# Keys and values of the first sequence finished at the attention's entry, a pool laid out first, and fewer column products ahead of and within the S5 tables

## The chip, the cores and the metric

The kernel runs on one NeuronCore of a Trainium2 chip. The metric is the device time of one execution in microseconds (us). The engines are named as in the profile: PE is TensorE (matmuls and transposes; PEld is its weight load), DVE is VectorE, ACT is ScalarE, POOL is GpSimd, and SP is SyncE, which here only issues transfers. Each engine works through its own queue in order. A transfer is issued by SP, ACT or POOL and runs on the core's 16 DMA engines.

## The reference

One encoder layer over two sequences of 512 tokens, width 1024, in float32. Each branch reads a normalized input; the two are gated and merged, and a squared-ReLU MLP follows.

```python
h = rms_norm(x, ln1)
q, k, v, u, g_att, g_ssm = jnp.split(h @ w_in, IN_SPLITS, axis=-1)   # 1024, 256, 256, 1024, 1024, 1024 columns
q = rms_norm(q.reshape(bsz, seq_len, 16, 64), q_gain)
k = rms_norm(k.reshape(bsz, seq_len, 4, 64), k_gain)
v = v.reshape(bsz, seq_len, 4, 64)
y_att = windowed_attention(q, k, v, sink, bias, mask)   # blocks of 128 queries, 3 blocks of keys, 16 heads on 4 key heads
y_ssm = s5_branch(u, ...)    # 64 groups of 16 channels, 64 complex states, forward and backward scan, then GELU and a gate
mixed = sigmoid(g_att) * y_att + sigmoid(g_ssm) * y_ssm
x = x + mixed @ w_out
return x + square(relu(rms_norm(x, ln2) @ w_up)) @ w_down
```

## The kernel before, in words

Every large product is made of three passes over operands that are split into a high part (a cast) and a low part (the difference): high by high, high by low, low by high. ScalarE makes the high part and VectorE the low one.

The part around the change has these stages, in order of time.

1. *Start (0 to about 60 us).* Keys and values of the first sequence are projected with the very first weights (strip_products) and stored, raw apart from the row's norm, in kv_scr (scaled_heads). The tokens are turned into hT. VectorE works out the powers pr and pi of the state matrix, which lie in the pool ssmc; the input rows, strips and bias line lie in the pool xin. From the powers, ScalarE and VectorE copy the arranged tables br_p, bi_p, er, ei (L518 to L526), and VectorE adds bs_p and es.
2. *Tables (to about 215 us).* tables(c) handles eight groups, in two steps of four. A step computes bpre (VectorE), turns it on TensorE (L608) into bm, computes ctab, and multiplies bm with the inputs u (L637), which fills the state array h. all_lags makes the Toeplitz lags.
3. *Recurrence (to about 358 us).* 62 steps of four VectorE operations (L737 to L740).
4. *Outputs (to about 430 us).* 32 quarter steps of small products (L771, L774) and a GELU.
5. *Attention's entry (about 441 to 470 us).* Four query tiles of the first head group are projected, and the values of the second sequence; the keys are turned. Then come the attention units.

Between these, TensorE is fed with the columns of the big projection (u and the two gates: 24 columns of 48 products of 128x512) and the second sequence's keys (96 products of 128x256). They stand in one generator; pull(n) issues the next n units of it at that place of TensorE's queue. A column product counts 2 units, a key product 1. Where the reserve "phase["units"] - 84" stands, so many units are left for after the last output. Each column's weights are cast (L182, c_hi) and subtracted (L183, c_lo) during the column before; the load of the next pair of raw halves (L172, c_raw) goes out once both are done. A gate column that ends in or before the recurrence gets its sigmoid with its evacuation; a later one gets a copy, and its sigmoid in a later stage.

During the recurrence the kernel also finishes the first sequence's keys and values, one block of 128 tokens after the other, in head_piece: from step 24 on, every second step, three pieces a block. Piece 0 loads the block from kv_scr (SP). Piece 1 squares the keys and casts the values (ScalarE), subtracts (POOL) and stores the values to v_scr (POOL's queue). Piece 2 reduces the squares (VectorE), adds the epsilon, takes the power -0.5 and scales the keys (POOL) and stores them to k_scr. Its three tiles per block (kv, kv_sq, va_t) share one ring of three slots:

```python
kv, sq = [sp.tile([P, 2, N_KV, HD], F32, tag="ys", name=n, bufs=3) for n in ("kv", "kv_sq")]
va_t = sp.tile([P, N_KV, P], F32R, tag="ys", name="va_t", bufs=3)
```

At the attention's entry, SP loads the finished keys (kn) and values (va), POOL copies the first head's keys twice side by side (kd, key_copies), and key_turn turns them after the first query tile. A query tile is projected, squared (ScalarE), reduced (VectorE), raised to -0.5 (POOL, power), scaled (VectorE, norm) and turned by TensorE one tile later; rows_block projects values between. Three PSUM banks ("acc") go round among projection, value rows and turned tile.

The order of work: in the start, all five engines follow the written order (manual_schedule). In the tables only TensorE and POOL do, VectorE, ScalarE and SP are ordered by a planner. In recurrence and outputs TensorE, ScalarE and VectorE follow the written order, POOL and SP the planner's. At the attention's entry only VectorE does. Pools lie on a stack: what is opened after a pool is closed takes its place in memory, and waits for it, tile by tile if the closed pool says reuse_waits="tile" (xin does, ssmc does not). The pools hst (the state array h) and ssmt (the tables' tiles, among them bcx, the coefficients that SP loads for each tables(c)) take the place of xin and ssmc. The line "line_scr" (L707) spreads the 16 bias lines over 128 partitions in DRAM; POOL issues it, after the loads of the first Toeplitz and output tables.

Of the kernel before, what the change touches and what calls it, by code (L numbers as in the profile page):

```python
# [19 lines left out]
P = 128  # L20
# [6 lines left out]
HALF = 512  # L27
# [36 lines left out]
def hybrid_layer(ctx, tc, x, x_t, w_kv, rel, onehot, w_qkv, w_ug, vectors, lam, coefs, w_glu, w_out, ln2,  # L64
# [39 lines left out]
    k_scr = dram.tile([P, NB, N_KV, HD], F32, name="k_scr")  # L104
    v_scr = dram.tile([P, NB, N_KV, P], F32, name="v_scr")
# [179 lines left out]
    with tc.tile_pool(name="xin", bufs=1, reuse_waits="tile") as xin, tc.tile_pool(name="ssmc", bufs=1) as sc:  # L285
# [232 lines left out]
        for src, e_t, b_t, eng in ((pr, er, br_p, S.copy), (pi, ei, bi_p, V.tensor_copy)):  # L518
            bt = b_t.rearrange("p g t -> p t g")
            eng(bt[0:64], src[0:64, 7::-1, :])  # L520
            eng(bt[64:128], src[64:128, 0:8, :])
# [7 lines left out]
        V.tensor_add(es, er, ei)  # L529
# [3 lines left out]
    with tc.tile_pool(name="hst", bufs=1) as hp:  # L533
# [11 lines left out]
        with tc.tile_pool(name="ssmt", bufs=2) as sp:  # L545
# [9 lines left out]
            def tables(c):  # L555
# [18 lines left out]
                for q in range(SB // SG):  # L574
# [40 lines left out]

                    tb = sp.tile([P, SG, 9, CH], F32, tag="tb", name="tb", bufs=1)
# [29 lines left out]
                    pull(48 if g0 + SG < GROUPS else 36)  # L646
# [21 lines left out]
            pull(96)  # L668
# [12 lines left out]
        with tc.tile_pool(name="ssmo", bufs=2) as sp:  # L681
# [28 lines left out]
            pieces = {}  # L710

            def head_piece(t, i):
                if i == 0:
                    kv, sq = [sp.tile([P, 2, N_KV, HD], F32, tag="ys", name=n, bufs=3) for n in ("kv", "kv_sq")]
                    va_t = sp.tile([P, N_KV, P], F32R, tag="ys", name="va_t", bufs=3)
                    pieces[t] = kv, sq[:, 0], va_t
                    SP.dma_start(kv, kv_scr[:, t])
                    return
                kv, sq, va_t = pieces[t]
                if i == 1:  # L720
                    S.activation(sq, kv[:, 0], AF.Square, scale=HD ** -0.5)
                    S.copy(va_t[:, :, 0:HD], kv[:, 1])
                    GP.tensor_tensor(va_t[:, :, HD:P], kv[:, 1], va_t[:, :, 0:HD].bitcast(F32), op=ALU.subtract)
                    GP.dma_start(v_scr[:, t], va_t.bitcast(F32))
                    return
                ms, rk = [small.tile([P, N_KV], F32, tag=tag, name=tag) for tag in ("ms", "rq")]
                V.reduce_sum(ms, sq, axis=AX.X)
                GP.tensor_scalar_add(ms, ms, EPS)
                GP.tensor_tensor(rk, ms, neg_half[:, 0:N_KV], op=ALU.pow)
                GP.tensor_tensor(kv[:, 0], kv[:, 0], rk[:, :, None].to_broadcast([P, N_KV, HD]), op=ALU.mult)  # L730
                GP.dma_start(k_scr[:, t], kv[:, 0])

            for i in range(1, NCHUNK - 1):
                if i >= 24 and i % 2 == 0 and (i - 24) % 8 < 6 and (i - 24) // 8 < NB:
                    head_piece((i - 24) // 8, (i - 24) % 8 // 2)
                t1, t2 = terms if i == 1 else [step_tile(n) for n in ("t1", "t2")]
                V.tensor_mul(t1, h[:, i], a8r)  # L737
                V.tensor_mul(t2, h[:, i, ::-1], a8i)
                V.tensor_add(t1, t1, h[:, i + 1])
                V.tensor_add(h[:, i + 1], t1, t2)  # L740
                pull(15)
# [19 lines left out]
            for q in range(GROUPS // SH):  # L761
# [23 lines left out]
                pull(-(-(phase["units"] - 84) // (GROUPS // SH - q)))  # L785
# [74 lines left out]
    with tc.tile_pool(name="att", bufs=2, reuse_waits="tile") as ap, tc.tile_pool(name="attc", bufs=1, reuse_waits="tile") as ac:  # L860
# [51 lines left out]

        def key_turn(j, sq, kd):
            kh = ap.tile([P, HALF], F32R, tag="kh", name="kh")
            kl = ap.tile([P, HALF], F32R, tag="kl", name="kl")
            keys[j, sq] = (kh, kl)
            ps = tps()
            for t in range(4):
                PE.transpose(ps[:, t * P:(t + 1) * P], kd[:, t].rearrange("p a d -> p (a d)"), ident)
            S.activation(kh, ps, AF.Copy, scale=gain_k)  # L920
            V.scalar_tensor_tensor(kl, ps, gain_k, kh.bitcast(F32), op0=ALU.mult, op1=ALU.subtract)
            queries[j, sq] = ap.tile([P, G, HALF], F32R, tag="qa", name="qa")
# [191 lines left out]
        with tc.manual_schedule(engines={ET.DVE}):  # L1114
            SP.dma_start(kn[:, 0:4], k_scr)
            kd = key_copies(0, 0)
            w_q = whole_block(w_qkv[Q_BLK], wq, "ya", 2)
            weights[0] = w_q
            w_v = whole_block(w_qkv[V_BLK], cpool, "p", 3)
            last_keys.pop()()  # L1120
            SP.dma_start(kn[:, 4:8], key_tiles[0])
            load_biases(0)
            SP.dma_start(va[:, 0:4].bitcast(F32), v_scr)
            rows = None
            for t in range(4):
                new = Tile(0, 0, t)
                new.project(3 * KT)
                new.square()
                new.power()
                new.norm()  # L1130
                if rows:
                    rows.turn()
                    rows.high()
                    rows.low()
                rows = new
                rows_block(w_v, NB + t, v_evac)
                if t == 0:
                    key_turn(0, 0, kd)
# [661 lines left out]
```

## Time and profile before

| what | value |
| --- | --- |
| median of 3 runs | 1485.83 us (1483.88 to 1486.2) |
| the profiled execution, whole | 1483.64 us |
| its span, first to last instruction | 1481.9 us |
| TensorE busy | 1441.8 us, 97% |
| VectorE busy | 1100.2 us, 74% |
| ScalarE busy | 765.2 us, 52% |
| GpSimd busy | 247.8 us, 17% |
| mean granted TensorE clock | 0.990 |

A group's row reads: line, engine, operation, output and inputs, shapes, count, then busy time and mean duration of one in ns, then idle time of the engine ahead of it and what ended it. A row of the timeline reads: start, duration, engine, line, operation, with idle time and releaser in brackets. A row of the waits reads: who, for whom, total us, times, longest. A row of a stretch reads: from and to, length, then busy time and instructions of each engine, then the granted clock of TensorE as a share of full speed, the DMA engines' busy share and GB/s. Matmul durations overlap in the rows, since they are pipelined; the spacing of their starts is their cost.

### The profile page before, as it was taken

To read this page: it belongs to the slowest core of one execution; us is meant where nothing else is said; L and a number is where in the kernel's file an instruction comes from. 1 tells how busy PE (TensorE), PEld (TensorE's weight loads), DVE (VectorE), ACT (ScalarE), POOL (GpSimd) and SP (SyncE) were. 2 spreads that over 40 slices of the span, in tenths; PEclk is the share of its full clock that TensorE was granted. 3 is DMA by queue.
4 is the path that set the end of the run, shared out by engine and by line. 5 is a ranking of instruction groups with operands and counts; after the bars stand their busy time and mean duration, and the time that the engine had idled before them with its cause. 6 is when DMAs were issued, how large, how long until landed. Compare 5 with 4: busy or idle time off the path is not lost.

```text
span 1481.9 us, 22085 instructions
## 1 busy us (share of the span) xinstructions
PE 1441.8 (97%) x7981; PEld 1227.5 (83%) x7981; DVE 1100.2 (74%) x1985; ACT 765.2 (52%) x1367; POOL 247.8 (17%) x408
## 2 busy tenths in 40 slices
PE   8899999779999999999999999999999999999998
PEld 7688888568999999987888878888888888888887
DVE  7889949678545899998995479777776588575653
ACT  7578872123435888787353255544444443433332
POOL 3034441322423433243100000000000000000000
PEclk9999999989999999999999999999999999999999
DMA  7255546653981342255554234444443794454441
GB/s 289 94 162 165 164 143 227 222 181 123 320 288 67 124 148 87 70 163 177 184 171 155 87 129 170 157 156 150 156 156 114 289 342 140 148 182 157 128 127 58
DMA packets 102524, 243.38 MB, mean 164 GB/s; under 512 B 12522, under 2 KB 24298, under 8 KB 102288
## 3 DMA queue, kind: packets, MB, share of 16 engines
q1 hardware_dynamic: 61968, 141.25, 29.4%
q0 software_dynamic: 16832, 49.86, 10.2%
q10 hardware_dynamic: 23616, 50.87, 9.3%
q8 instruction: 63, 1.03, 0.3%
q14 instruction: 45, 0.37, 0.1%
HBM read 170.60 MB, written 83.39 MB: 171 GB/s over the span
## 4 chain that ended last, share of the span: by engine, by line
PE 65%; DVE 8%; ACT 3%; DMA 2%; issue 2%; POOL 1%; SPq 0%; DVEq 0%; ACTq 0%; POOLq 0%
PE bank L123 13%; PE bank L124 13%; PE bank L125 13%; PE acc L937 5%; PE acc L125 2%; PE acc L123 2%; PE acc L124 2%; PE acc L130 2%; PE sps L774 2%; PE po L1020 2%; PE acc L192 2%; PE sps L988 2%; PE tps L1004 2%; DMA k_scr<-kv 1%; PE sps L771 1%
## 5 line engine op out<-in xcount | busy, mean ns | idle before, releaser
L192 PE MATMUL acc<-act,c_hi 128*128 128x512 f32 x768 | 245.6, 400 | 19.5 <-ACT c_hi L182 19.5
L192 PEld LDWEIGHTS acc<-act,c_hi 128*128 128x128 f32 x768 | 142.7, 191 | 48.0 <-ACT c_hi L182 20.3
L124 PE MATMUL bank<-b_lo,a_hi 128*128 128x512 f32 (+1 forms) x449 | 174.4, 389 | 0.0
L125 PE MATMUL bank<-b_hi,a_lo 128*128 128x512 f32 (+1 forms) x449 | 174.4, 389 | 0.0
L123 PE MATMUL bank<-b_hi,a_hi 128*128 128x512 f32 (+1 forms) x449 | 174.4, 389 | 0.0
L192 PE MATMUL acc<-act,c_lo 128*128 128x512 f32 x384 | 151.7, 395 | 0.2 <-DVE c_lo L183 0.2
L1656 ACT CAST a_hi<-d_a 128x1024 fp32r<-128x1024 f32 x56 | 59.0, 1054 | 177.3 <-PE bank L124 174.1
L123 PE MATMUL bank<-act,act 128*128 128x512 f32 x368 | 143.2, 389 | 0.3 <-DVE tx L1444 0.3
L124 PE MATMUL bank<-act,act 128*128 128x512 f32 x368 | 143.2, 389 | 0.0
L125 PE MATMUL bank<-act,act 128*128 128x512 f32 x368 | 143.2, 389 | 0.0
L1657 DVE TENSOR_TENSOR a_lo<-d_a,a_hi 128x1024 fp32r<-128x1024 f32 x56 | 68.5, 1223 | 95.9 <-ACT a_hi L1656 95.9
L937 PE MATMUL acc<-w_hi,act 128*128 128x256 f32 x512 | 114.2, 291 | 0.7 <-ACT w_hi L1108 0.7
L125 PEld LDWEIGHTS bank<-b_hi,a_lo 128*128 128x128 f32 x449 | 84.3, 188 | 17.5
L123 PEld LDWEIGHTS bank<-b_hi,a_hi 128*128 128x128 f32 x449 | 84.3, 188 | 17.4
L124 PEld LDWEIGHTS bank<-b_lo,a_hi 128*128 128x128 f32 x449 | 84.3, 188 | 17.3
L937 PEld LDWEIGHTS acc<-w_hi,act 128*128 128x128 f32 x512 | 87.0, 189 | 4.6 <-ACT w_hi L1108 0.9
L192 PEld LDWEIGHTS acc<-act,c_lo 128*128 128x128 f32 x384 | 73.0, 190 | 16.0 <-DVE c_lo L183 1.0
L998 ACT ACTIVATE p<-p,nmx 128x257 f32<-128x257 f32 (+1 forms) x128 | 72.1, 564 | 19.7 <-DVE nmx L992 17.4
L123 PEld LDWEIGHTS bank<-act,act 128*128 128x128 f32 x368 | 69.1, 188 | 15.0 <-issue 0.6
L130 PE MATMUL acc<-act,gc_hi 128*128 128x512 f32 x256 | 81.0, 394 | 0.0
L124 PEld LDWEIGHTS bank<-act,act 128*128 128x128 f32 x368 | 69.1, 188 | 14.4
L125 PEld LDWEIGHTS bank<-act,act 128*128 128x128 f32 x368 | 69.1, 188 | 14.2
(358 smaller groups left out, 3434.6 us busy)
## 6 DMA issues: line engine op xcount, KB each, us to landing
d_a<-a_scr SPq DMA_DIRECT2D x56, 512.0 KB, 3.6
raws<-in_w_up_dram SPq DMA_DIRECT2D x32, 512.0 KB, 4.0
a_scr<-t ACTq DMA_DIRECT2D x64, 256.0 KB, 2.8
k<-in_w_down_dram SPq DMA_DIRECT2D x32, 512.0 KB, 6.4
c_raw<-in_w_ug_dram SPq DMA_DIRECT2D x48, 256.0 KB, 3.7
ct_scr<-ctab POOLq DMA_DIRECT2D x16, 512.0 KB, 4.4
ctab_in<-ct_scr POOLq DMA_DIRECT2D x16, 512.0 KB, 7.1
a_scr<-a ACTq DMA_DIRECT2D x32, 256.0 KB, 2.0
```

Of the source, the lines that this page charges most:

```text
L123: PE.matmul(ps, a[0], b[0], start=first, stop=False)
L124: PE.matmul(ps, a[0], b[1], start=False, stop=False)
L125: PE.matmul(ps, a[1], b[0], start=False, stop=last)
L130: PE.matmul(ps, w[wi][:, k, :], rows[yi], start=k + p == 0, stop=k == KT - 1 and p == 2)
L192: PE.matmul(ps, w[wi][:, k, :], hT[s][hi][:, k, :], start=n == 0, stop=n == 3 * KT - 1)
L774: PE.matmul(o, ctab[:, g0 % SI + g, ri, 0:T * CH], st[:, ri, g].rearrange("p s k -> p (s k)"), start=False, stop=ri == 1)
L937: PE.matmul(self.ps, hT[sq][act][:, k, col:col + P], w[:, k % 4, :], start=i == 0, stop=i == 3 * KT - 1)
L988: PE.matmul(ps[:, 0:self.nk], qs, kk[:, self.k0 * P:self.k1 * P], start=i == 0, stop=i == 1)
L998: S.activation(p, p, AF.Exp, bias=self.nmx[:, h:h + 1], scale=-1.0, accum_out=self.sums[:, h, self.qb:self.qb + 1])
L1004: PE.transpose(pt[:, h * P:(h + 1) * P], self.p[:, h, 1 + i * P:1 + (i + 1) * P], ident)
L1656: S.copy(hi, src)
L1657: V.tensor_sub(lo, src, hi.bitcast(F32))
```

## The change

The pieces in the recurrence, k_scr and v_scr go. At the attention's entry the raw keys and values come straight from kv_scr: the four blocks' keys are squared, reduced, raised and scaled in one operation each, the values cast and subtracted in one each; the copy kd moves behind the first tile's value rows, and key_turn behind the third's. The pool ssmc is opened ahead of xin, so that it lies below it. The arranging copies are dealt anew (ScalarE gives one half of br_p to VectorE), and es is added in the first step of the tables. The pulls become 72 for 96 ahead of the tables and 44 for 48 in fifteen of their sixteen steps; the reserve behind the outputs becomes 100 for 84.

```diff
-    k_scr = dram.tile([P, NB, N_KV, HD], F32, name="k_scr")
-    v_scr = dram.tile([P, NB, N_KV, P], F32, name="v_scr")
...
-    with tc.tile_pool(name="xin", bufs=1, reuse_waits="tile") as xin, tc.tile_pool(name="ssmc", bufs=1) as sc:
+    with tc.tile_pool(name="ssmc", bufs=1) as sc, tc.tile_pool(name="xin", bufs=1, reuse_waits="tile") as xin:
...
-        for src, e_t, b_t, eng in ((pr, er, br_p, S.copy), (pi, ei, bi_p, V.tensor_copy)):
+        for src, b_t, engs in ((pr, br_p, (S.copy, V.tensor_copy)), (pi, bi_p, (V.tensor_copy,) * 2)):
             bt = b_t.rearrange("p g t -> p t g")
-            eng(bt[0:64], src[0:64, 7::-1, :])
-            eng(bt[64:128], src[64:128, 0:8, :])
+            engs[0](bt[0:64], src[0:64, 7::-1, :])
+            engs[1](bt[64:128], src[64:128, 0:8, :])
...
-        V.tensor_add(es, er, ei)
...
+                    if g0 == 0:
+                        V.tensor_add(es, er, ei)
                     tb = sp.tile([P, SG, 9, CH], F32, tag="tb", name="tb", bufs=1)
...
-                    pull(48 if g0 + SG < GROUPS else 36)
+                    pull(44 if g0 + SG < GROUPS else 36)
...
-            pull(96)
+            pull(72)
...
-            def head_piece(t, i):
...
             for i in range(1, NCHUNK - 1):
-                if i >= 24 and i % 2 == 0 and (i - 24) % 8 < 6 and (i - 24) // 8 < NB:
-                    head_piece((i - 24) // 8, (i - 24) % 8 // 2)
...
-                pull(-(-(phase["units"] - 84) // (GROUPS // SH - q)))
+                pull(-(-(phase["units"] - 100) // (GROUPS // SH - q)))
...
+        def query_tile(j, sq):
+            if (j, sq) not in queries:
+                queries[j, sq] = ap.tile([P, G, HALF], F32R, tag="qa", name="qa")
...
-            SP.dma_start(kn[:, 0:4], k_scr)
-            kd = key_copies(0, 0)
+            SP.dma_start(kn[:, 0:4], kv_scr[:, :, 0])
...
-            SP.dma_start(va[:, 0:4].bitcast(F32), v_scr)
+            vn = ap.tile([P, NB, N_KV, HD], F32, tag="p", name="vn", bufs=3)
+            SP.dma_start(vn, kv_scr[:, :, 1])
+            k_sq = evp.tile([P, NB, N_KV, HD], F32, tag="ev", name="k_sq")
+            ms, rk = [small.tile([P, NB * N_KV], F32, tag="rsum", name=n, bufs=2) for n in ("k_ms", "k_rs")]
+            query_tile(0, 0)
             rows = None
             for t in range(4):
                 new = Tile(0, 0, t)
                 new.project(3 * KT)
+                if t == 0:
+                    S.activation(k_sq, kn[:, 0:4], AF.Square, scale=HD ** -0.5)
+                    V.reduce_sum(ms, k_sq.rearrange("p t h d -> p (t h) d"), axis=AX.X)
+                    GP.tensor_scalar_add(ms, ms, EPS)
+                    GP.tensor_tensor(rk, ms, neg_half, op=ALU.pow)
                 new.square()
                 new.power()
                 new.norm()
...
                 rows_block(w_v, NB + t, v_evac)
                 if t == 0:
+                    V.tensor_mul(kn[:, 0:4], kn[:, 0:4],
+                                 rk.rearrange("p (t h) -> p t h", t=NB)[:, :, :, None].to_broadcast([P, NB, N_KV, HD]))
+                    kd = key_copies(0, 0)
+                if t == 1:
+                    S.copy(va[:, 0:4, :, 0:HD], vn)
+                    V.tensor_sub(va[:, 0:4, :, HD:P], vn, va[:, 0:4, :, 0:HD].bitcast(F32))
+                if t == 2:
                     key_turn(0, 0, kd)
```

More of the change, by code (lines that the diff above doesn't have):

```diff
@@ L709, in hybrid_layer @@
             order.enter_context(tc.manual_schedule(engines={mybir.EngineType.PE, mybir.EngineType.Activation, mybir.EngineType.DVE}))
-            pieces = {}
-            def head_piece(t, i):
[L713 to L731, printed above, removed]
             for i in range(1, NCHUNK - 1):
-                if i >= 24 and i % 2 == 0 and (i - 24) % 8 < 6 and (i - 24) // 8 < NB:
-                    head_piece((i - 24) // 8, (i - 24) % 8 // 2)
                 t1, t2 = terms if i == 1 else [step_tile(n) for n in ("t1", "t2")]
@@ L921, in key_turn @@
             V.scalar_tensor_tensor(kl, ps, gain_k, kh.bitcast(F32), op0=ALU.mult, op1=ALU.subtract)
-            queries[j, sq] = ap.tile([P, G, HALF], F32R, tag="qa", name="qa")
+            query_tile(j, sq)
         class Tile:
```

## The prediction

> **What bounds the kernel now.** I read the page first: TensorE is nearly the whole span, so only its gaps, and the time it runs at half clock, can be won; work that merely moves along its queue wins nothing. The waits of TensorE come next (total, times, longest, in us).
>
> ```profile
> PE 1441.8 (97%) x7981; PEld 1227.5 (83%) x7981; DVE 1100.2 (74%) x1985; ACT 765.2 (52%) x1367; POOL 247.8 (17%) x408
> ...
> PE acc L192 <- ACT c_hi L182: 19.5, 2, 18.9
> PE tps L608 <- issue: 3.7, 1, 3.7
> ...
> PE sps L774 <- ACT st L750: 0.9, 1, 0.9
> ...
> PE acc L937 <- ACT w_hi L1108: 0.7, 1, 0.7
> ...
> PE acc L937 <- DVE w_lo L1109: 0.3, 1, 0.3
> ```
>
> One wait is 18.9 us. The timeline around it, one piece of the chain that ended last, and the table of transfers say what it is:
>
> ```profile
> 272.49 0.41 DVE L727 TENSOR_REDUCE ms<-kv_sq 128x4 f32<-128x256 f32 x1
> 273.00 0.32 POOL L728 TENSOR_SCALAR ms<-ms 128x4 f32<-128x4 f32 x1 [11.78 <-DVE ms L727]
> ...
> 285.83 0.39 PE L192 MATMUL acc<-act,c_lo 128*128 128x512 f32 x1
> 285.90 1.05 POOL L707 DMA_DIRECT2D line_scr<-line_one  x1 [1.39 <-DMA u_sb<-u_scr]
> ...
> 289.02 0.62 POOL L731 DMA_DIRECT2D k_scr<-kv  x1 [0.30 <-POOL kv L730]
> ...
> 304.17 0.40 ACT L722 CAST va_t<-kv 128x256 fp32r<-128x256 f32 x1 [25.86 <-DMA k_scr<-kv]
> 305.13 1.41 DVE L183 TENSOR_TENSOR c_lo<-c_raw,c_hi 128x512 fp32r<-128x512 f32 x2 [20.14 <-ACT c_hi L182]
> ...
> 289.02 15.07 DMA k_scr<-kv
> ...
> line_scr<-line_one POOLq DMA_DIRECT2D x1, 4096.0 KB, 17.9
> ```
>
> The second head piece's cast (va_t) waits for a slot of the three-deep "ys" ring, held until the first piece's keys are stored. That store left POOL at 289.02, behind the 4 MB bias-line copy of 285.90, and took 15.07 us. ScalarE runs in order, so the column weights' cast c_hi stood behind va_t; TensorE stopped for want of c_hi, and VectorE for the same reason (20.14 us). The next view gives busy time by engine, then granted clock, in four stretches.
>
> ```profile
> 289.53:305.05 15.52, 0.00 (x0) 0.00 (x0) 0.00 (x0) 0.88 (x3) 0.50 (x2) 0.50 0.86 299
> 305.05:310.01 4.96, 4.86 (x12) 3.66 (x13) 4.78 (x12) 2.17 (x5) 2.32 (x5) 0.50 0.58 199
> 65.30:68.95 3.65, 0.00 (x0) 0.03 (x1) 2.83 (x6) 3.03 (x11) 0.00 (x0) 0.82 0.56 186
> 224.25:285.00 60.75, 60.75 (x270) 50.30 (x269) 58.17 (x147) 11.77 (x21) 14.68 (x22) 1.00 0.60 197
> ```
>
> After the stop TensorE ran 4.96 us at clock 0.50. The last row gives the price of a column product: 60.75 us by 270 is 0.225 us.
>
> **The change, part by part.** All sums are against the profiled execution's own 1483.64 us (span 1481.9); the median of the runs, 1485.83, stands 2.2 above it.
>
> *Head pieces out of the recurrence.* Gone are four SP loads, eight ScalarE, four VectorE and sixteen POOL operations, and eight POOL stores. No ring slot waits for a store any more, so the 18.9 us stop goes, and with it the half clock behind it, worth half of 4.96: 2.5 us. Together 21.4. What is late next? VectorE's recurrence runs beside these products; it gains 20.14 us of idle time and the reduces:
>
> ```profile
> L727 DVE TENSOR_REDUCE ms<-kv_sq 128x4 f32<-128x256 f32 x3 | 1.2, 411 | 0.0
> ```
>
> That is 21.3, as much as TensorE gains, so the two arrive together at the outputs as before; of the 0.9 us wait on st there I take 0.5 as won (between 0 and 0.9). POOL is no longer held until VectorE's reduce of 272.49, so the table loads and the bias-line copy go out earlier, beside the column loads (a rival below).
>
> *Fewer columns ahead.* The 24 units ahead of the tables are 12 products, the 4 units in 15 steps are 30: 42 products, 9.5 us, move into the output stage, where TensorE works without gaps as well. By itself nothing (one half column's sigmoid more falls to the later stage, on a ScalarE that is busy for 52% of the span), provided that the tables still cover VectorE. Seven pairs of steps from 80.42 to 204.37 sum to:
>
> ```profile
> sum 123.95, PE 123.95 PEld 108.31 DVE 112.51 ACT 101.55 POOL 54.90; mean PE 17.71 PEld 15.47 DVE 16.07 ACT 14.51 POOL 7.84
> ...
> 88.81 1.28 DVE L598 TENSOR_TENSOR bpre<-tb,bpre 128x512 f32<-128x512 f32 x2
> ...
> 89.98 1.04 PE L608 MATMUL tps<-ident,bpre 128*128 128x128 f32 x8
> ```
>
> A pair takes TensorE 17.71 us; four products fewer make it 16.81, still over VectorE's 16.07. Only the third step has no slack (VectorE ends at 90.09, the transposes start at 89.98); it may lose up to 1.8 (two steps' 0.9, doubled for a late one). I take 0, since VectorE also starts earlier, by the next part.
>
> *Powers' pool first, copies dealt anew, es later.*
>
> ```profile
> 55.04 1.16 ACT L521 COPY br_p<-pr 64x512 f32<-64x512 f32 x1
> ...
> 56.78 0.66 DVE L520 COPY bi_p<-pi 64x512 f32<-64x512 f32 x1
> ...
> 58.23 0.69 DVE L522 TENSOR_TENSOR bs_p<-br_p,bi_p 128x512 f32<-128x512 f32 x1
> ...
> 59.53 0.24 ACT L526 COPY er<-pr 128x64 f32<-128x64 f32 x1
> ...
> 59.84 0.80 SPq L560 DMA_DIRECT2D bcx<-in_coefs_dram  x2
> ...
> 62.76 0.43 DVE L566 TENSOR_TENSOR tw<-bcx,fi 128x256 f32<-128x256 f32 x1 [0.89 <-DMA bcx<-in_coefs_dram]
> ...
> 68.95 0.66 PE L608 MATMUL tps<-ident,bpre 128*128 128x128 f32 x2 [3.67 <-issue]
> ```
>
> The bcx load leaves at 59.84, right behind the last copy out of the powers (59.53 plus 0.24): its place lies over their pool. With that pool at the bottom, bcx lies over the input pool, whose tiles come free one by one, and it can land well ahead. VectorE takes one more copy (0.66), so bs_p ends near 59.6; two c_lo (1.3) first, tw starts at 60.9 at the latest instead of 62.76, at best at 59.6. It took 6.2 us from tw to the transposes, part of it waiting: they start between 64.0 and 67.1; I take 65.4. ScalarE has 1.16 less. Gained are 68.95 - 65.4 = 3.55, less 12 products that are no longer done by then (2.7): 0.85. The half clock that follows shows in two stretches:
>
> ```profile
> 68.90:72.00 3.10, 1.99 (x9) 1.62 (x9) 3.06 (x5) 2.14 (x9) 0.00 (x0) 0.50 0.32 113
> 72.00:75.00 3.00, 3.00 (x11) 2.39 (x10) 2.75 (x5) 0.86 (x2) 0.15 (x1) 0.59 0.00 0
> ```
>
> That is 1.99 us of work at half rate and, at a mean of 0.59, 2.46 more: half of 4.45 is 2.2. I count 0.65 of it, since about 3 us of idle time are left. Taken: 1.5, between -0.9 (67.1) and 5.5 (64.0, its half clock and the second short wait gone). The es addition falls beside transposes.
>
> The Trainium skill ("TensorE: Matmul & The Clock Gate", Part 1) has the clock drop only after an idle window of about 3.4 us, free-running; by that alone the entry might keep the full clock, and the sum would be 1.5 us lower. The trace is less kind: in the 3.65 us from 65.30 the mean clock is 0.82, so it fell 2.3 us after the last product.
>
> *The tail.* 100 units instead of 84 are left behind the outputs, 16 key products of half a column's width: by halving 0.225, 1.8 us more cover for the weights of the first queries. The waits of 0.7 and 0.3 go: 1.0 (0 if the loads shift along).
>
> *Attention's entry.* Added: a 1024-wide square and a 1024-wide copy on ScalarE, a reduce, a product and a difference of 1024 on VectorE, an addition and a power of 16 columns on POOL; the kd copy and the key turn come later; SP's va load (1 MB) becomes vn (512 KB), kn comes from 1 KB runs. TensorE has no gap from 445 to 470, so it decides whether the first tile's norm comes late:
>
> ```profile
> 447.62 0.41 DVE L947 TENSOR_REDUCE ms<-sq 128x4 f32<-128x256 f32 x1
> ...
> 449.50 0.42 DVE L954 TENSOR_TENSOR qn<-acc,rq 128x256 f32<-128x256 f32 x1 [1.47 <-POOL rq L950]
> ...
> 451.94 0.60 PE L959 MATMUL acc<-ident,qn 128*64 128x128 f32 x4
> ...
> L308 POOL TENSOR_TENSOR factors<-ss,neg_half 128x1 f32<-128x1 f32 x8 | 4.6, 581 | 0.7
> ...
> L950 POOL TENSOR_TENSOR rq<-ms,neg_half 128x4 f32<-128x4 f32 x32 | 33.2, 1037 | 2.7
> ...
> L1657 DVE TENSOR_TENSOR a_lo<-d_a,a_hi 128x1024 fp32r<-128x1024 f32 x56 | 68.5, 1223 | 95.9 <-ACT a_hi L1656 95.9
> ```
>
> qn has 2.0 us of slack before its turn (449.92 to 451.94). VectorE's order is written out: the keys' reduce comes ahead of the tile's, about 1.2 us by the 1223 ns row. POOL then raises 16 columns: from 581 ns for one and 1037 for four, 152 ns a column, so 2.9 us (at least 1.04, at most four times 1.04). The keys' power ends near 452.0, the tile's 1.3 later, qn near 453.8; with the key turn gone from ahead TensorE is there at 451.6 and waits 2.2. The keys' product (1.2) delays the second round by another 0.7. Cost 2.9, between 0.4 and 5. Queued behind: v_evac's difference and the bank that the next projection needs.
>
> **The sum.** 21.4 + 0.5 + 1.5 + 1.0 - 2.9 = 21.5: 1483.6 - 21.5 = 1462.
>
> **Rivals.** (1) Collision: loads and the bias-line copy move into busy columns. Speaks for it: a column load took as long as 10.0 us.
>
> ```profile
> DMA to landing us min/median/max: 2.5/3.5/10.0
> ```
>
> Against: from fetch to cast lie 42 products (9.5 us), and 44 more (9.9) until TensorE needs them, so a load must exceed 19 us; at 17.9 + 10.0 one stop of 8.5 and its 2.5 of clock follow: 1473. That the stop comes back with another cause, so that the change does not do what it says, is this case. (2) The tables come to hang on VectorE (16.07 against 16.81 is thin): up to 9.5 us of new gaps, 1471.5. (3) The entry's 2.2 us wait falls so that the clock halves for another 6.8 us: 3.4 more, 1465.5. The cited section would let a wait that short pass. (4) The other side: the keys' reduce stands at the head of VectorE's written order, and the lows, norms and evacuations of the entry stand behind it; if kn lands late, all wait. Before, POOL's copy had kn here, 8 us before the 447.6 at which the reduce would stand:
>
> ```profile
> 439.45 0.61 POOL L910 COPY kd<-kn 128x512 f32<-128x512 f32 x1 [1.45 <-DMA kn<-k_scr]
> ```
>
> It decides from about 28 us of lateness (8 of slack, less the square's 1, and 21.5 of gain); at 35 the time is 1490. No landing quoted exceeds 17.9.
>
> **How the numbers follow.** Forecast 0.78; collision 0.07, tables 0.05, clock 0.06, late keys 0.03, the rest 0.01. The bounds give 1455 (21.4 + 0.9 + 5.5 + 1.0 - 0.4 = 28.4) and 1470 (21.4 - 0.9 - 1.8 - 5 = 13.7). This range takes in the clock rival and leaves out 0.16. Faster by over 0.2% (3 us; what a measurement of this kernel tells from none): 0.96; within 0.01; slower 0.03.
>
> **What would show it.** Right: no wait on c_hi over 1 us in the recurrence, clock 1.00 through it; bcx issued before 59; first transposes near 65; table pairs of 16.8 us with TensorE unbroken; a 16-column power near 2.9 us and a TensorE wait on qn of 1 to 3 us at the entry. Wrong: a wait on c_hi with a column load behind it, gaps at the transposes, or a wait at the entry beyond 5 us.

## The result and the profile after

The changed kernel takes 1468.66 us (median of 4 runs, 1467.71 to 1470.89), the kernel before beside it 1484.88 (1483.88 to 1486.2): a ratio of 0.9892, with a 95% interval of 0.9875 to 0.991. It is 16.2 us faster. The forecast was 1462, with a range of 1455 to 1470: the direction and the range held, and 5 to 7 us of the forecast gain of 21.5 did not come (5.3 by the medians, 6.6 by the profiled executions). The profiled executions differ by 14.9 us (1483.64 and 1468.74; the span after is 1467.0).

The first row of the page after the change:

```profile
PE 1441.2 (98%) x7981; PEld 1228.4 (84%) x7981; DVE 1099.3 (75%) x1985; ACT 764.4 (52%) x1361; POOL 234.2 (16%) x386
```

The waits of TensorE after the change (who, for whom, total us, times, longest), from the second on; its first, at the start of the kernel, stood in the kernel before too:

```profile
PE tps L605 <- issue: 4.9, 1, 4.9
PE acc L915 <- DVE keys L247: 3.8, 1, 3.8
PE acc L937 <- DVE qn L932: 3.0, 2, 2.9
```

TensorE is as busy as before, so what was won was idle time: 1481.9 - 1441.8 = 40.1 us before, 1467.0 - 1441.2 = 25.8 after. The 18.9 us wait on c_hi is gone, the waits on st and on the first query weights too. Two are new, both at the attention's entry: 3.8 us on a key tile (line 247, the second sequence's keys), and 2.9 on qn. A row of busy time by stretch, from the end of the tables to the last outputs, shows that nothing took the place of the stop:

```profile
225.00:400.00 175.00, 175.00 (x955) 151.50 (x954) 136.68 (x298) 58.10 (x98) 33.02 (x48) 1.00 0.67 231
```

TensorE worked through all 175 us, at a granted clock of 1.00.

The timeline of the tables' entry, where bcx now leaves 6 us earlier:

```profile
53.81 0.81 SPq L557 DMA_DIRECT2D bcx<-in_coefs_dram  x2
...
60.59 0.69 DVE L520 TENSOR_TENSOR bs_p<-br_p,bi_p 128x512 f32<-128x512 f32 x1
...
66.00 2.10 PE L605 MATMUL tps<-ident,bpre 128*128 128x128 f32 x8 [4.88 <-issue]
```

The transposes start at 66.00 instead of 68.95. The wait ahead of them is longer, 4.88 us for 3.67, since 12 products fewer stand there; the second one, of 1.06, is gone, and so are two short waits for the columns' weights that the kernel before had at 60.35 and 61.32 (0.54 and 0.24 us). And the attention's entry, where the loss is:

```profile
405.96 0.33 ACTq L214 DMA_DIRECT2D gs_scr<-sg  x1
...
416.13 1.06 ACT L1110 ACTIVATE k_sq<-kn 128x1024 f32<-128x1024 f32 x1 [6.41 <-DMA gs_scr<-sg]
...
421.77 0.55 PE L915 MATMUL acc<-w_hi,act 128*128 128x256 f32 x1 [3.84 <-DVE keys L247]
...
428.45 1.21 DVE L1111 TENSOR_REDUCE k_ms<-k_sq 128x16 f32<-128x1024 f32 x1
...
430.10 2.93 POOL L1113 TENSOR_TENSOR k_rs<-k_ms,neg_half 128x16 f32<-128x16 f32 x1
...
434.50 0.42 DVE L932 TENSOR_TENSOR qn<-acc,rq 128x256 f32<-128x256 f32 x1 [4.51 <-POOL rq L928]
...
434.98 0.73 PE L937 MATMUL acc<-ident,qn 128*64 128x128 f32 x4 [2.88 <-DVE qn L932]
```

The square of the keys (k_sq) takes a slot of the two-deep evacuation ring "ev". That slot still held the tile sg of a gate column, whose store to gs_scr was issued at 405.96 and took 10.2 us to land; ScalarE stood 6.41 us for it with the key tiles' own squares (line 239) behind it in its order, so a PSUM bank came free late and TensorE waited 3.84 us. Later the 16-column power keeps POOL for 2.93 us, the tile's own power stands behind it, and TensorE waits 2.88 us for qn. Each of the two waits was followed by a stretch at half clock. Busy time and granted clock in windows of 3.41 us, laid from 418.31:

```profile
418.31:421.72 3.41, 0.00 (x0) 0.00 (x0) 2.16 (x6) 3.41 (x9) 1.64 (x2) 1.00 0.88 283
421.72:425.13 3.41, 3.36 (x16) 3.39 (x17) 1.94 (x5) 1.37 (x2) 1.26 (x2) 0.50 0.31 114
...
431.95:435.36 3.41, 0.54 (x6) 0.36 (x4) 0.86 (x3) 0.38 (x1) 2.35 (x3) 1.00 0.28 108
435.36:438.77 3.41, 3.41 (x19) 3.39 (x17) 1.52 (x3) 0.68 (x1) 1.88 (x3) 0.50 0.00 0
```

Both half-clock stretches fill exactly one window and cost half of it, 1.7 us each.

### The profile page after: what moved, and what is told of

Same layout as the page of the kernel before. It is cut to its first block, busy times and chain, and to the rows that moved or that the text cites. A ratio compares the mean times of both kernels' runs of the same rounds, so it can differ in the third digit from the quotient of the medians.

```text
span 1467.0 us, 22018 instructions
## 1 busy us (share of the span) xinstructions
PE 1441.2 (98%) x7981; PEld 1228.4 (84%) x7981; DVE 1099.3 (75%) x1985; ACT 764.4 (52%) x1361; POOL 234.2 (16%) x386
## 4 chain that ended last, share of the span: by engine, by line
PE 85%; DVE 6%; DMA 3%; ACT 2%; issue 2%; POOL 1%; SPq 0%; DVEq 0%; ACTq 0%; POOLq 0%
PE acc L190 17%; PE bank L121 13%; PE bank L122 13%; PE bank L123 13%; PE acc L915 5%; PE acc L123 2%; PE acc L121 2%; PE acc L122 2%; PE acc L128 2%; PE sps L636 2%; PE po L998 2%; PE sps L748 2%; PE sps L966 2%; PE tps L982 2%; PE acc L343 1%
## 5 line engine op out<-in xcount | busy, mean ns | idle before, releaser
L123 PEld LDWEIGHTS bank<-act,act 128*128 128x128 f32 x368 | 69.1, 188 | 14.5
```

The lines of the kernel that those rows point to most:

```text
L123: PE.matmul(ps, a[1], b[0], start=False, stop=last)
```

## The experiments

All times are medians, beside the kernel before on the same chip (1484.9 to 1485.9 each time); ratios are to that kernel, with their 95% interval in brackets. The intervals reach some 0.0015 to either side, so two versions that lie less than about 3 us apart are not told apart by the times alone; there the waits decide.

### The two waits at the entry

**Another ring for the square.** The edit to the changed kernel:

```diff
-            k_sq = evp.tile([P, NB, N_KV, HD], F32, tag="ev", name="k_sq")
+            k_sq = ap.tile([P, NB, N_KV, HD], F32, tag="qa", name="k_sq")
```

> The changed kernel with the squared keys (k_sq) in the ring of the query tiles (qa) instead of the two-slot ring "ev", nothing else. Slot theory: ScalarE's 6.41 us of idle time ahead of the keys' square is the wait for the last gate column's store to leave its "ev" slot; it goes, and with it TensorE's 3.8 us wait on the second sequence's keys and the 3.4 us at half clock behind it (1.7 us): 1468.7 - 5.5 = 1463. Rival (ScalarE's added work and its order): the square still stands ahead of the key tiles' squares, the wait stays at 3 us or more, 1467 to 1469.

1465.98 us (1462.51 to 1466.53), ratio 0.9867 (0.9851 to 0.9883): by the medians 2.7 less than the changed kernel. Of its waits of TensorE one is left at the entry:

```profile
PE acc L937 <- DVE qn L932: 3.4, 2, 3.3
```

The wait on the key tile is gone, so the slot was its cause. The clock did not give back its part: the wait on qn alone, now 3.3 us, was followed by two half-clock windows, of which the first is shown (busy time by engine, then granted clock; in the second, TensorE worked throughout, at 0.50). That is the profiled execution; the other three of this version had a mean granted clock of 0.997 to 0.998 against its 0.995, so fewer such windows.

```profile
426.81:430.22 3.41, 1.36 (x12) 1.15 (x10) 0.00 (x0) 0.38 (x1) 3.24 (x3) 1.00 0.52 169
430.22:433.63 3.41, 2.21 (x11) 2.10 (x12) 2.29 (x4) 0.68 (x1) 1.29 (x2) 0.50 0.01 3
```

**The keys' power behind the first tile's norm.** The square, reduce, addition and power of the keys move behind the tile's:

```diff
+                new.square()
+                new.power()
+                new.norm()
                 if t == 0:
                     S.activation(k_sq, kn[:, 0:4], AF.Square, scale=HD ** -0.5)
...
-                new.square()
-                new.power()
-                new.norm()
```

> The changed kernel with the keys' square, reduce, addition and 16-column power moved behind the first query tile's norm, nothing else. Power theory: TensorE's 2.9 us wait on qn at the entry is the 2.9 us power standing ahead of the tile's own on POOL; it goes with the 1.7 us of half clock behind it: 1468.7 - 4.6 = 1464, and lower (to 1459) if the planner now also places the square behind the key tiles' squares on ScalarE. Rival (VectorE's 1024-wide work is what delays): the wait moves to the second tile's norm, and the time stays at 1467 or more.

1471.18 us (1470.38 to 1471.86), ratio 0.9906 (0.9892 to 0.9921): no gain; by the medians 2.5 more. As the rival said, the wait on qn of the first tile became one on qn of the second, and the slot's wait is now counted against the weights' cast behind it (waits of TensorE):

```profile
PE acc L915 <- DVE qn L932: 3.8, 1, 3.8
PE acc L915 <- ACT w_hi L1086: 3.1, 1, 3.1
```

**Both together.**

> Both edits together: if the two waits are separate, 1468.7 - 5.5 - 4.6 = 1458.6. If one wait only hid the other, about 1463.

1467.42 us (1465.23 to 1468.44), ratio 0.9879 (0.9865 to 0.9894). The diff is that of the two before it. The two waits it was made to end did not both go, and neither time came: one wait of 3.8 us on qn is left. The timeline tells why:

```profile
430.56 2.93 POOL L1116 TENSOR_TENSOR k_rs<-k_ms,neg_half 128x16 f32<-128x16 f32 x1
433.52 1.23 DVE L1124 TENSOR_TENSOR kn<-kn,k_rs 128x1024 f32<-128x1024 f32 x1 [3.07 <-POOL k_rs L1116]
...
436.96 0.42 DVE L932 TENSOR_TENSOR qn<-acc,rq 128x256 f32<-128x256 f32 x1 [1.88 <-POOL rq L928]
...
437.44 0.39 PE L915 MATMUL acc<-w_hi,act 128*128 128x256 f32 x1 [3.79 <-DVE qn L932]
```

VectorE follows the written order here. The keys' scaling product (line 1124) stands after the power's 2.93 us, and VectorE waits 3.07 us in front of it with the second tile's reduce and norm behind. Wherever the chain of reduce, power and product stands among the tiles, its 5.6 us (1.21, 0.27, 2.93 and 1.23) fall into somebody's turn.

**The keys' chain ahead of all the entry.** The square (in the other ring), reduce, addition and power are written first, right after the load of kn:

```diff
             SP.dma_start(kn[:, 0:4], kv_scr[:, :, 0])
+            k_sq = ap.tile([P, NB, N_KV, HD], F32, tag="qa", name="k_sq")
...
+            S.activation(k_sq, kn[:, 0:4], AF.Square, scale=HD ** -0.5)
+            V.reduce_sum(ms, k_sq.rearrange("p t h d -> p (t h) d"), axis=AX.X)
+            GP.tensor_scalar_add(ms, ms, EPS)
+            GP.tensor_tensor(rk, ms, neg_half, op=ALU.pow)
```

> The changed kernel with the squared keys in the qa ring, and the keys' square, reduce, addition and power written first at the attention's entry, ahead of the weights' lows (the scaling product stays where it is). Theory (both entry waits are the power's and the square's place in their queues): both go with 3.4 us of half clock: 1468.7 - 10.1 = 1458.6. Rival (the 2.9 us power now delays the second sequence's key tiles on POOL, whose PSUM banks TensorE needs): 1461 to 1465, with a wait on keys or on their banks.

1463.94 us (1462.72 to 1466.25), ratio 0.9858 (0.9843 to 0.9873): by the medians 4.7 less than the changed kernel and, with one below, the lowest of all. Its timeline:

```profile
411.52 2.94 POOL L1099 TENSOR_TENSOR k_rs<-k_ms,neg_half 128x16 f32<-128x16 f32 x1
...
415.94 0.42 DVE L247 TENSOR_TENSOR keys<-acc,rk 128x256 f32<-128x256 f32 x1 [3.43 <-POOL rk L244]
```

Its waits of TensorE at the entry:

```profile
PE acc L230 <- DVE keys L247: 1.5, 1, 1.5
...
PE acc L915 <- DVE keys L247: 0.4, 1, 0.4
```

The power now delays a key tile's own power (line 244), which costs TensorE 1.5 us, as the rival said; the 0.4 is on the last key tile, some 10 us later. No half clock follows. So of the two waits and their clock, 10.1 us in the changed kernel, waits of 1.9 us are left and the rest was a matter of order and of the ring; the time fell by less than the difference of 8.2, by 4.7 (medians) or 6.0 (profiled executions), and why is open.

### The parts of the change alone

**Only the move to the entry** (tables' pulls, reserve and pools as before):

```diff
-                if i >= 24 and i % 2 == 0 and (i - 24) % 8 < 6 and (i - 24) // 8 < NB:
-                    head_piece((i - 24) // 8, (i - 24) % 8 // 2)
...
+            SP.dma_start(kn[:, 0:4], kv_scr[:, :, 0])
```

> The kernel before with only the move of the keys and values to the attention's entry (pools, copies, pulls and reserve as before). Theory (this part carries the gain and the losses at the entry): 21.4 + 0.9 us gained, 4.6 to 9 lost at the entry: 1485.9 - 22.3 + 4.6 to 9 = 1468 to 1472.5. Rival (pulls and layout carry 4 us or more of the 16): 1474 or more.

1467.22 us (1465.61 to 1468.1), ratio 0.9877 (0.9862 to 0.9892). The move alone carries the whole gain of the change, a little more than the theory's 1468 to 1472.5 allowed: the stop on c_hi is gone (0.6 us are left). With 84 units of reserve there is no wait on a key tile, and one on qn of 2.6 us with one half-clock window.

**Only the pool, the copies and es:**

```diff
+    with tc.tile_pool(name="ssmc", bufs=1) as sc, tc.tile_pool(name="xin", bufs=1, reuse_waits="tile") as xin:
...
+            engs[0](bt[0:64], src[0:64, 7::-1, :])
+            engs[1](bt[64:128], src[64:128, 0:8, :])
```

> The kernel before with only the powers' pool laid first, the copies dealt anew and es added later (pulls as before). Theory (the earlier first transposes are worth something only while 96 units cover the wait): the transposes start near 66 instead of 69, the gap shrinks from 3.7 + 1.1 to about 2.2 us: 3 us faster, 1482.9, and 1480.7 if the half clock goes too. Rival (the part is worth the 1 us seen in the changed kernel whatever the pull): 1484 to 1485.

1482.34 us (1479.7 to 1484.47), ratio 0.9979 (0.997 to 0.9989), as forecast. With the 96 units still ahead of them, the transposes start at 67.06 after a wait of 2.07:

```profile
67.06 1.67 PE L607 MATMUL tps<-ident,bpre 128*128 128x128 f32 x8 [2.07 <-issue]
```

The two waits there shrink from 4.7 to 3.5 us, and the two short waits for the columns' weights (0.54 and 0.24) are gone: 2.0 us. The half clock lasts one window instead of two, but the second held idle time: the work at half clock falls from 4.45 us to 3.41, which is worth half of the difference, 0.5. That is about 2.5 of the 3.3 us between the medians. The two profiled executions themselves differ by only 0.3 us (spans 1481.9 and 1481.6), since other waits were longer in this one, among them the first of the kernel, 6.3 us for 5.4. The stop on c_hi stays, 19.5 us.

**Only the three numbers** (72, 44, and 100 in reserve):

```diff
-                    pull(48 if g0 + SG < GROUPS else 36)
+                    pull(44 if g0 + SG < GROUPS else 36)
...
-            pull(96)
+            pull(72)
...
-                pull(-(-(phase["units"] - 84) // (GROUPS // SH - q)))
+                pull(-(-(phase["units"] - 100) // (GROUPS // SH - q)))
```

> The kernel before with only the pulls 72 and 44 and the reserve 100. Theory (moved products are worth nothing, and 12 fewer ahead of the first transposes lay that wait bare): 2.7 us more gap there, 1.0 less at the tail: 1485.9 + 1.7 = 1487.6. Rival (fewer products in the tables let VectorE set the pace): 1490 or more. Rival (they shorten the time): 1484 or less.

1484.28 us (1483.5 to 1486.61), ratio 0.9993 (0.9983 to 1.0002): no difference, where about 2 us of loss was expected. The gap at the transposes did grow, and the stop shrank:

```profile
PE acc L192 <- ACT c_hi L182: 17.9, 2, 17.3
PE tps L608 <- issue: 6.1, 1, 6.1
```

That is 2.4 us more in front of the transposes and 1.6 less on c_hi, and the waits on the first query weights are gone. Fewer columns ahead show no gain by themselves in the kernel before.

The three parts alone gained 18.4, 3.3 and 1.4 us by the medians, 23.1 together, and the whole change 16.2: they do not add up. What the whole has and none of the parts is the wait on the key tile with its half clock, 5.5 us; below, it goes when the reserve alone is put back.

### The cause of the stop

**The bias-line copy ahead of the tables**, in the kernel before, with the pieces still in the recurrence:

```diff
+            GP.dma_start(line_scr, line_one[:, None, :].to_broadcast([N_HEADS, P, LINE]))
             pending = []
             pull(96)
...
-            GP.dma_start(line_scr, line_one[:, None, :].to_broadcast([N_HEADS, P, LINE]))
```

> The kernel before with one line moved: the 4 MB bias-line copy is issued ahead of the tables instead of behind the first output tables. Queue theory (the 15 us store of the keys is the line copy ahead of it in POOL's queue): the 18.9 us stop on c_hi goes with its half clock, 1484.9 - 21.4 = 1463.5, the head pieces staying in the recurrence. Rival (the three-slot ring and POOL's late stores do it by themselves): a stop of 10 us or more stays, 1475 or more. Second rival (the copy collides with the first table loads): the stop goes, but the gap at the first transposes grows, 1465 to 1472.

1482.79 us (1481.24 to 1484.92), ratio 0.9979 (0.9969 to 0.9988). Its first two waits of TensorE:

```profile
PE tps L608 <- DMA c_raw<-in_w_ug_dram: 12.4, 1, 12.4
PE acc L192 <- ACT c_hi L182: 7.2, 2, 6.7
```

The first piece's addition in the timeline, and a piece of the chain that ended last:

```profile
283.07 0.33 POOL L728 TENSOR_SCALAR ms<-ms 128x4 f32<-128x4 f32 x1 [11.31 <-DVE ms L727]
...
296.51 5.71 DMA k_scr<-kv
```

With the copy away, the first piece's store of keys, the one that ScalarE waits for, lands in 5.71 us instead of 15.07, and the stop falls from 18.9 to 6.7 us: about two thirds of it were the copy. The rest is POOL's own lateness: it waits for VectorE's reduce until 283.07, and then issues the store of the values and ten loads ahead of the power, so that the store of keys leaves only at 296.51.

The copy in its new place collided with the column loads: a wait of 12.4 us at the transposes. So the time is what the first rival said, 1475 or more, but by the way of the second: the collision took back most of what the stop gave. It is a collision of the kind that the prediction's first rival describes; in the changed kernel the copy is issued at 242.46, and nothing waited.

### The reserve and the columns ahead

**The changed kernel with 84 units in reserve:**

```diff
-                pull(-(-(phase["units"] - 100) // (GROUPS // SH - q)))
+                pull(-(-(phase["units"] - 84) // (GROUPS // SH - q)))
```

> The changed kernel with one number put back: 84 units instead of 100 kept behind the outputs. In the changed kernel ScalarE held the square of the keys for 6.41 us, because its slot in the two-deep evacuation ring was still owned by the last gate column's tile, and TensorE then waited 3.8 us for the key tile behind it; where the move to the entry was made alone, with 84 units, that wait was absent. Theory (the wider reserve moves the last gate column, and so its store, 3.6 us later, up against the keys' square): the wait of 3.8 us on the key tile goes, a short wait on the query weights of about 1 us comes back, and half a 3.4 us stretch at half clock may go too: 1464 to 1466. Rival (the reserve only moves work along the queue, and the slot is late with any reserve): the wait stays within 1 us of 3.8, and the time within 1 us of 1468.7.

1466.37 us (1465.83 to 1467.73), ratio 0.9874 (0.9857 to 0.989): by the medians 2.3 less than the changed kernel. Beside the wait on qn (2.6 us), TensorE has one on the first query weights:

```profile
PE acc L915 <- DVE w_lo L1087: 1.6, 2, 1.3
```

The timeline:

```profile
405.21 0.33 ACTq L214 DMA_DIRECT2D gs_scr<-sg  x1
...
409.99 0.63 SPq L1093 DMA_DIRECT2D kn<-kv_scr  x1
...
413.03 2.59 SPq L878 DMA_DIRECT2D bias<-line_scr  x4
...
414.79 1.06 ACT L1110 ACTIVATE k_sq<-kn 128x1024 f32<-128x1024 f32 x1 [2.08 <-DMA kn<-kv_scr]
```

The wait on the key tile is gone, as the theory had it, but not by the theory's way. The store left at 405.21, only 0.75 us earlier than with 100. What differs is SP's order. In the changed kernel it has:

```profile
403.96 0.63 SPq L1093 DMA_DIRECT2D kn<-kv_scr  x1
...
407.13 9.79 SPq L878 DMA_DIRECT2D bias<-line_scr  x4
```

There the loads of kn, the query weights and the bias go out beside the store, which takes 10.2 us to land; with 84 units they go out later, and it takes 2.7. So the slot is free before the keys' square wants it, and the square waits for kn instead, with two key tiles' squares ahead of it instead of one. The other versions agree: with 100 units the bias loads leave within 3 us behind the store, which takes 7.0 to 10.6 us; with 84 they leave more than 7 us behind it, and it takes 2.7 to 3.3. No run moves these loads alone, so that they slow the store is argued from the order and not shown. SP and ScalarE are ordered by the planner at the entry.

**The hoisted version with 84 units:**

```diff
-                pull(-(-(phase["units"] - 100) // (GROUPS // SH - q)))
+                pull(-(-(phase["units"] - 84) // (GROUPS // SH - q)))
```

> The version with the square, reduce, addition and power of the first sequence's keys written first at the entry and with the square's slot in another ring (1463.9), now with 84 units instead of 100 kept behind the outputs. The slot is no longer an issue, so the reserve shows only its own worth. Theory of the prediction (the 16 key products of the reserve cover the conversion of the first query weights, 1.0 us): waits of TensorE on the highs and lows of those weights of 0.7 and 0.3 come back, 1464.9. Rival (the loads shift along with the products): no such wait, 1463.9 or slightly less, since the keys' square comes sooner than the key tiles need VectorE.

1468.09 us (1466.42 to 1470.53), ratio 0.9884 (0.9869 to 0.9899): slower than with 100 by 4, which neither theory had. The timeline:

```profile
412.20 0.64 SPq L1093 DMA_DIRECT2D kn<-kv_scr  x1
...
418.79 1.06 ACT L1096 ACTIVATE k_sq<-kn 128x1024 f32<-128x1024 f32 x1 [4.67 <-DMA kn<-kv_scr]
...
421.54 3.27 POOL L1099 TENSOR_TENSOR k_rs<-k_ms,neg_half 128x16 f32<-128x16 f32 x1
...
426.26 0.42 DVE L247 TENSOR_TENSOR keys<-acc,rk 128x256 f32<-128x256 f32 x1 [4.24 <-POOL rk L244]
...
427.34 0.58 PE L915 MATMUL acc<-w_lo,act 128*128 128x256 f32 x1 [4.29 <-DVE w_lo L1087]
```

Here the late load of kn hurts: ScalarE stands 4.67 us for it, and the keys' power comes so late that it meets a key tile's own power. VectorE waits 4.24 us for that tile, with the lows of the query weights (w_lo) behind it in its written order, and TensorE waits 4.29 us for them. It is the prediction's fourth rival on a small scale. So the reserve's worth is not a cover of 1.0 us: it decides where the planner puts the loads, and so which engine is held by what.

**The hoisted version with 96 and 48 units ahead:**

```diff
-                    pull(44 if g0 + SG < GROUPS else 36)
+                    pull(48 if g0 + SG < GROUPS else 36)
...
-            pull(72)
+            pull(96)
```

> The same version (keys' work first at the entry, square in another ring, 100 units kept) with 96 and 48 column units ahead of and within the tables, as before, instead of 72 and 44. Theory (with the powers' pool first the tables' entry still needs 2 to 3 us more cover than 72 units give, and each of the 12 products put back covers 0.225 us of it): the wait of 4.8 us ahead of the first transposes falls to 2 to 3.5 us in all, the half clock there from 6.8 to 3.4 us, so 1.5 to 2.5 from the wait and 1.7 from the clock, no new wait in the tables: 1460 to 1461.5. Rival (the 42 products only move, and the start of the tables is set by VectorE and the coefficients' load, which the extra columns delay on ScalarE and VectorE): 1463 to 1465.

1463.54 us (1463.08 to 1465.67), ratio 0.9855 (0.984 to 0.987): the same as with 72 and 44 (0.9858). The place behaved as the theory said:

```profile
PE tps L605 <- issue: 2.1, 1, 2.1
...
PE tps L605 <- DVE bpre L595: 1.4, 1, 1.4
```

That is 3.5 us for 4.8, with one half-clock window for two. Yet the time is the rival's. The half clock was worth little (work of 3.41 us at half rate for 3.96), small waits came elsewhere (0.8 on a table's load, 0.6 on ys), and TensorE's busy time was 1.5 us higher. Of this, 0.8 arose before 47 us, where the edit changes nothing: the clock of the first products rose at 10.42 us instead of 8.54. The rest stays open.

**Both numbers put back.** This version had a third difference: 24 units more were issued between recurrence and outputs.

> The same version with both put back: 96 and 48 column units, and 84 kept. If the two numbers act on separate places, the time is that of the version with 96 and 48 plus the difference that the reserve alone made: 1460 to 1462.5. Rival (they are tied: more units early mean fewer left behind the tables, and the last gate column, the query weights and the entry come closer together): a new wait of 1 us or more at the attention's entry, 1463 or more.

1468.09 us (1465.97 to 1468.51), ratio 0.988 (0.9865 to 0.9895), with the same wait of 4.3 us on w_lo as the hoisted version with 84. The rival's time and wait came, but not for its reason: by the medians 84 units cost 4.5 us here and 4.2 with 72 and 44, so their effect shows no tie to the columns ahead.

## Why the prediction held, and where it did not

- *The stop and its clock, 21.4 us:* right. The part alone gained all of it, and no wait and no half clock is left between 225 and 400 us. The cause named (a store behind the 4 MB copy on POOL's queue) was about two thirds of it; the rest was POOL's lateness, its wait for VectorE and the loads it issued first.
- *The wait on st, 0.5:* 0.9; it is gone.
- *The tables' entry, 1.5:* about 1.3 (68.95 - 66.00 = 2.95, less the 2.7 of twelve products, plus the second wait of 1.06). But the step to it was partly wrong: bs_p ended at 61.3, not near 59.6, because the planner set other work on bcx between the copies, the transposes came at 66.0 and not 65.4, and the half clock that was to lose 0.65 stayed at two windows. What made up for it was the second short wait, which was in the upper bound alone, and the two waits on the columns' weights, which the prediction did not count.
- *The tail, 1.0:* the waits on w_hi and w_lo are gone, also in the version with the square in another ring, where no wait on a key tile could hide them, and came back with 84 units (1.6). The reason given was too simple, as the two versions with 84 show.
- *The tables, 0:* right; TensorE worked 144.30 of the 145 us from 80 to 225, as this row shows, so the rival of VectorE did not come.

```profile
80.00:225.00 145.00, 144.30 (x1275) 125.09 (x1275) 120.88 (x243) 110.11 (x161) 67.63 (x119) 1.00 0.55 168
```

- *The attention's entry, -2.9:* this is the step that failed. It measured -10.1: waits of 3.84 and 2.88 us and two half-clock windows of 1.7. The power was sized right (2.93 against 2.9), and the wait on the first tile's qn, taken as 2.2 with 0.7 for the second round, was 2.88. Missing was the wait of 3.84: the prediction followed the square's duration on ScalarE, but not the ring slot that it writes to. Its words "No ring slot waits for a store any more" hold for the recurrence, and the change itself put a new tile into another ring whose slot a store held. Missing from this term, too, was the clock. The 10.1 lie far outside the term's own bounds of 0.4 to 5; that the time still fell inside the range is luck, since the range's far end took losses in other terms that did not come.
- *The clock rival:* it came. Its price, 3.4 us, was right by luck: it spoke of one stretch of two windows behind the wait on qn, and in the changed kernel one of the two windows stands behind the slot's wait. Without the slot's wait (the square in another ring) it came as described, two windows behind qn, and that version took 1465.98, close to the rival's 1465.5.

The terms as measured, 21.4 + 0.9 + 1.3 + 1.0 - 10.1, give 14.5 us, against the 14.9 between the two profiled executions.

## What to carry to other kernels

When a step is moved, write down for each of its tiles which ring it takes its slot from, who held that slot last, and whether a store must land before it is free; a duration alone does not show that. A long operation on a side engine (here a power of 2.93 us) belongs where no tile's own short chain follows within that time: moved behind one tile it met the next; written first it cost 1.5 us of waiting, but 4.3 where its load came late. Where a planner orders some of the queues, a change of one number elsewhere can move a load past others, so compare the order of the queues, not only the waits.

## What the runs showed of the hardware

The clock of TensorE was decided in windows of 3.41 us, and a window did not have to be idle to halve the next one. Every stretch at half clock between the first products and the last, in the fourteen profiled executions, was 3.41 us long or a multiple of it, up to 20.48. In the changed kernel the two drops, at 421.72 and 435.36, lie 13.64 us apart, four windows, and a window with 0.54 us of work was followed by half clock. In the hoisted version with 96 and 48 units, at the transposes, one with 1.37 was too (busy time by engine, then granted clock):

```profile
65.03:68.44 3.41, 1.37 (x10) 1.12 (x11) 3.41 (x6) 1.78 (x8) 0.00 (x0) 1.00 0.75 223
68.44:71.86 3.42, 3.42 (x10) 2.65 (x9) 3.42 (x6) 3.33 (x13) 0.00 (x0) 0.50 0.28 77
```

The version with both numbers put back had the same two waits at the transposes, 2.1 and 1.4 us, and kept its full clock there. Counted back from its drop at 421.20 in steps of 3.41, its windows there lie otherwise, and the emptiest of them still held about 2 us of work:

```profile
66.25:69.66 3.41, 2.01 (x12) 1.67 (x13) 3.41 (x6) 2.63 (x10) 0.00 (x0) 1.00 0.52 159
```

The windows of the other executions, laid back from their drops in the same way, fall apart at about half: at full clock, none with 1.59 us of work or less kept it, and none with 1.77 or more lost it. The two nearest are these, from the version with the three numbers alone, where the clock fell, and from the one with the pool, the copies and es alone, where it stayed:

```profile
61.25:64.67 3.42, 1.59 (x6) 0.67 (x4) 2.50 (x8) 0.76 (x3) 0.00 (x0) 1.00 0.83 244
...
283.15:286.57 3.42, 1.77 (x8) 1.13 (x6) 0.50 (x2) 0.00 (x0) 2.05 (x2) 1.00 1.03 377
```

At half clock more work was needed to rise: windows with up to 2.63 us were followed by another at half clock, and the clock rose only behind windows with 3.06 or more. So a wait of 2 to 3 us cost 1.7 us on top or nothing, by where it fell in the windows. The Trainium skill ("TensorE: Matmul & The Clock Gate", Part 1) has a free-running window of 3413 ns, and with that the traces agree; it has the clock fall after an idle window, and there they differ: 1.59 us of work in a window did not keep it. The prediction took the Trainium skill's rule as a reason to doubt the clock rival, and the runs decide against it.
